# Moving one of three PSUM evacuations of the attention from ScalarE to VectorE, and removing dead parts of the expert value sums

## The chip, the cores and the metric

One core of a Trainium2 chip runs the whole layer in one launch. The metric is the device time of the execution in microseconds (us), of which the median of several runs is taken. A profile is one execution with the hardware profiler on; its span runs from the first to the last instruction.

## What is computed

The reference is one layer of a hybrid backbone over 1024 tokens of width 1024, in float32, with 256 context tokens. The parts that matter here, cut from it:

```python
def one_block(qblk):                       # grouped-query attention: 8 heads, 2 key/value heads, 1280 keys
    s = jnp.einsum('bqkgd,btkd->bkgqt', qblk, k) * scale
    p = jax.nn.softmax(s.astype(jnp.float32), axis=-1).astype(v.dtype)
    return jnp.einsum('bkgqt,btkd->bqkgd', p, v)
...
def chunk(xc):                             # PEER: 128 tokens, 8 heads, the best 16 of 16384 experts per head
    ...
    eidx = jnp.take_along_axis(cidx, pos, axis=-1)
    g = jax.nn.softmax(best, axis=-1)
    a = jnp.einsum('chkd,cd->chk', u_tab[eidx], xc)
    wgt = (jax.nn.gelu(a.astype(jnp.float32)) * g).astype(xc.dtype)
    return jnp.einsum('chk,chkd->cd', wgt, v_tab[eidx])
```

Around them stand a modulated RMSNorm, one input projection, a long convolution (Hyena) beside the attention, gates, an output projection, and a final RMSNorm.

## The kernel before

Tokens lie on 128 partitions, in 8 tiles of 128. The program is written in stages, and a scheduler orders each engine's instructions by simulating a timeline, so stages overlap and one edit can reorder every engine behind it. Each engine then works its own list strictly in that order. The stages and when the trace shows them:

- to 660 us: conditioning, norms, key/value projection, the filters of the convolution, the query projection, and the columns of the convolution and the gates (`hcols`);
- to 870 us: the convolution (`hyena`, lines 180 to 285), of which each spectrum is a block of matmuls and then some twenty VectorE operations (lines 209 to 234);
- 680 to 1200 us: the attention (`attn`, lines 600 to 655), first between the convolution's matmuls, then alone, and from about 940 us between the matmuls of `rest` for tiles 0 to 3 (merge, output projection, expert queries), which fill TensorE;
- 1140 to 1860 us: `rest` for tiles 4 to 7, the selection of the best experts (`topk`), and the dense gate matrices of tiles 0 to 4 (`gbuild`);
- from 1740 us to the end: `dense`, where for tiles 0 to 4 all 16384 experts are computed by matmul, in 32 chunks. Between its steps runs `background`, where tiles 5 to 7 gather their 128 rows of U per token (`usweep`), multiply and reduce them on VectorE, and then gather and add 128 rows of V (`vrows`).

The attention in detail. A step takes one token tile and a pair of heads, one of each key/value head. For each head TensorE computes scores `sc` in three PSUM blocks (line 622), VectorE takes their maxima (`m`, `nmx`, lines 623 and 624), ScalarE exponentiates into `pr` (line 627), TensorE transposes `pr` in groups of 4, 4 and 2 blocks of 128 keys into a PSUM tile `pt` (line 633), and ScalarE copies each group to `pT` in SBUF (line 634). `pt` has two buffers (`npt` is 2), so a third group waits until the first is copied out. Twenty matmuls (line 640) then sum the values, and VectorE copies the result to `aT` (line 641). With 64 heads times tiles there are 192 copies, three per head.

The experts of tiles 5 to 7. `topk(..., False)` ends with the chosen experts' numbers `ef` as floats. Line 855 transposes them on TensorE into the one-buffer PSUM tile `ms`, line 858 casts `ef` to the integers `ei`, which the gathers of lines 887 and 933 use, and line 860 casts the transposed numbers to `eT`. `eT` is read only in `vsweep` (lines 897 to 925), which `background` makes only for a tile outside `VD`; `VD` is (5, 6, 7), which is all of them. So `vsweep` is never run, and the tile `wdz` that it uses is set aside in SBUF and never written. In `topk` a multiplication by `ce` (line 840, GpSimd) stands between a comparison (`eq`, line 839) and a sum (`ef`, line 841) on VectorE.

Of the kernel before, what the change touches and what calls it, by code (L numbers as in the profile page):

```python
# [10 lines left out]
F32 = mybir.dt.float32  # L11
F32R = mybir.dt.float32r
I32 = mybir.dt.int32
# [4 lines left out]
PSUM = bass.MemoryType.PSUM  # L18
# [3 lines left out]
D = 1024  # L22
# [33 lines left out]
CH, WB, VH, GA, UR = 4, 4, 4, 1, 1  # L56
# [8 lines left out]
VD = (5, 6, 7)  # L65
# [4 lines left out]
def body(tc, d, out, dbg=None):  # L70
# [22 lines left out]
    with es:  # L93
# [506 lines left out]
        def attn(tiles, kT, vt, hsel, p, ps, nsc):  # L600
            npt = 2
            blks = ((0, 512), (512, 1024), (1024, 1280))
            for ti in tiles:
# [9 lines left out]
                for h2 in range(4):  # L613
                    pTs = []
                    for kv in range(2):
# [13 lines left out]
                        for k0 in range(0, 10, 4):  # L629
                            nk = min(4, 10 - k0)  # L630
                            pt = ps.tile([128, 512], F32, name="pt", bufs=npt)
                            for m in range(nk):
                                PE.transpose(pt[:, m * 128:(m + 1) * 128], pr[:, (k0 + m) * 128:(k0 + m + 1) * 128], ident)
                            S.copy(pT[:, k0:k0 + nk, :], pt[:, :nk * 128].rearrange("p (m t) -> p m t", m=nk))
# [165 lines left out]
        def topk(i, v16, i16, p, res, ps, dense):  # L800
# [53 lines left out]
            pt = ps.tile([128, 512], F32, name="ms")  # L854
            PE.transpose(pt[:, 0:128], efl, ident)
            if not dense:
                ei = res.tile([128, 128], I32, name=f"ei{i}", bufs=1)
                V.tensor_copy(ei, efl)
                eT = res.tile([128, 128], I32, name=f"eT{i}", bufs=1)
                V.tensor_copy(eT, pt[:, 0:128])  # L860
                tops[i] = gwl, ei, eT
                return
            PE.transpose(pt[:, 128:256], gwl, ident)
# [33 lines left out]
        def vsweep(i, tops, ws, p, gp, ms, ap, res, wdz):  # L897
            w, eT = ws[i], tops[i][2]
            pt = ms.tile([128, 512], F32, name="ms")
            PE.transpose(pt[:, :128], w, ident)  # L900
            acc = ap.tile([128, 2, 512], F32, name="acc")
            pv = pt[:, :128].rearrange("p (c t) -> p c t", c=4)
            wT = res.tile([128, 4, 32], F32, name="wT", bufs=1)
            V.tensor_copy(wT, pv)
            for th in range(8):
                V.memset(wdz, 0.0)
                V.tensor_copy(wdz[:, :, th * 4:128:33], wT[:, :, th * 4:th * 4 + 4])
                for tm in range(4):
                    tl = th * 4 + tm
                    vgs = [gp.tile([128, D], F32, name="row", bufs=RW) if c else p.tile([128, D], F32, name="vg", bufs=VB) for c in range(4)]  # L910
                    for c in range(4):
                        G.indirect_dma_start(out=vgs[c], out_offset=None, in_=d["v"], in_offset=bass.IndirectOffsetOnAxis(ap=eT[:, c * 32 + tl:c * 32 + tl + 1], axis=0))
                    lead = None
                    for h in range(2):
                        for c in (3, 0, 1, 2):
                            mm = PE.matmul(acc[c * 32:c * 32 + 32, h, :], wdz[:, c, tm * 32:tm * 32 + 32], vgs[c][:, h * 512:(h + 1) * 512],
                                           start=tl == 0, stop=tl == 31, tile_position=(0, c * 32))
                            if lead is None:
                                lead = mm
                            else:  # L920
                                tc.add_manual_dep(mm.ins, lead.ins.name, mybir.DependencyInfo(mybir.DependencyClass.NoSync, mybir.DependencyReason.DATA), reason="behind the last gather")
                    yield 1
            gt = [gp.tile([128, D], F32, name="row", bufs=RW) for _ in range(4)]
            gates(gt)
            final(i, acc.rearrange("p a b -> p (a b)"), gt[2], gt[3], gt, p)

# [373 lines left out]
```

## Time and profile before

| | |
|---|---|
| median of 3 runs | 3746.49 us (3746.31 to 3755.15) |
| the profiled execution | 3752.46 us |
| its span | 3750.7 us |
| mean granted TensorE clock | 0.949 |
| TensorE (PE) matmul busy | 3369.1 us, 90% |
| VectorE (DVE) busy | 2879.9 us, 77% |
| ScalarE (ACT) busy | 1445.1 us, 39% |
| GpSimd (POOL) busy | 1709.2 us, 46% |

Shares are means over stages with different limits, so a stage is read from its own stretch. A row of the waits names the waiting engine with its tile and line, then what released it, then the sum of the idle time, the number of waits and the longest. A row of instruction groups gives busy time and the mean length of one in ns, and after the second bar the idle time of that engine just before them. PE is TensorE's matmuls, PEld its weight loads. An arrow points from what is read to what is written, and names stand without their numbers.

### The profile page before, as it was taken

The numbers are of one execution on the slowest core, as the hardware profiler recorded it, in microseconds if no ns is written. First come the engines' busy times: TensorE is split into PE (matmuls) and PEld (weight loads), VectorE is DVE, ScalarE is ACT, GpSimd is POOL, SyncE is SP. The second block draws the span as 40 slices with busy tenths as digits, with TensorE's granted clock in tenths as the row PEclk, the third lists the DMA queues.
The fourth block names the chain that finished last, engine by engine and source line by source line (L and its number), as shares of the span: only waits on it lengthen the run. The fifth ranks groups of instructions, "written<-read, shape, count | busy, mean of one in ns | idle before, by whom it ended". The sixth has DMA issues, their size and how long they took to land.

```text
span 3750.7 us, 53277 instructions
## 1 busy us (share of the span) xinstructions
PE 3369.1 (90%) x19601; PEld 2948.2 (79%) x19601; DVE 2879.9 (77%) x5428; ACT 1445.1 (39%) x2966; POOL 1709.2 (46%) x1360
## 2 busy tenths in 40 slices
PE   5899999789999886998889998999999999799998
PEld 2787888567887676888778888988888888687887
DVE  4655554574446899999897989898898989787777
ACT  5543422446565268885511222222232222122222
POOL 0233133220421465104486767676576666544452
PEclk6999999899999998999989999999999999899999
DMA  4554355863322344434488999999999989888886
GB/s 164 176 165 153 129 202 167 294 226 117 110 85 65 104 141 163 167 141 142 165 305 307 322 327 329 337 344 324 335 342 331 325 317 326 286 286 285 264 281 210
DMA packets 334241, 868.31 MB, mean 232 GB/s; under 512 B 31777, under 2 KB 145377, under 8 KB 324764
## 3 DMA queue, kind: packets, MB, share of 16 engines
q0 software_dynamic: 123904, 453.04, 33.9%
q1 hardware_dynamic: 210076, 411.87, 32.4%
q8 instruction: 154, 2.52, 0.3%
q14 instruction: 107, 0.88, 0.1%
HBM read 777.63 MB, written 87.18 MB: 231 GB/s over the span
## 4 chain that ended last, share of the span: by engine, by line
DVE 23%; DMA 16%; PE 14%; issue 8%; POOL 3%; ACT 2%; SPq 0%; DVEq 0%; POOLq 0%; ACTq 0%
PE mm L85 5%; PE mm L86 4%; PE mm L87 4%; DMA vg<-in_v,ei 4%; DMA vr<-in_v 3%; DVE row L888 3%; DVE acc L937 3%; DMA row<-in_u,ei 3%; DMA ur<-in_uT 3%; DVE o L953 2%; DVE o L965 2%; DVE wl L91 1%; DMA h<-in_v,ei 1%; DVE o L963 1%; POOL row L887 1%
## 5 line engine op out<-in xcount | busy, mean ns | idle before, releaser
L85 PE MATMUL mm<-h2Th,uh 128*128 128x320 f32 x2048 | 644.7, 315 | 60.7 <-ACT uh L90 50.3
L87 PE MATMUL mm<-h2Th,ul 128*128 128x320 f32 x2048 | 638.5, 314 | 26.7 <-DVE ul L91 25.8
L86 PE MATMUL mm<-h2Tl,uh 128*128 128x320 f32 x2048 | 641.7, 314 | 0.0
L887 POOL DMA_INDIRECT row<-in_u,ei x384 | 500.4, 1303 | 192.9 <-issue 75.3
L85 PE MATMUL mm<-vh,wh 128*128 128x512 f32 x1280 | 500.6, 404 | 59.6 <-DVE acc L1022 35.9
L888 DVE SCALAR_TENSOR_TENSOR row<-row,h 128x1024 f32<-128x1024 f32 x384 | 508.1, 1341 | 25.1 <-DMA row<-in_u,ei 21.7
L86 PE MATMUL mm<-vl,wh 128*128 128x512 f32 x1280 | 504.3, 401 | 5.8 <-DVE vl L91 3.9
L87 PE MATMUL mm<-vh,wl 128*128 128x512 f32 x1280 | 497.4, 400 | 7.6 <-DVE wl L91 7.5
L85 PEld LDWEIGHTS mm<-h2Th,uh 128*128 128x128 f32 x2048 | 392.9, 192 | 68.6 <-ACT uh L90 56.0
L933 POOL DMA_INDIRECT vg<-in_v,ei x255 | 310.6, 1218 | 295.8 <-DVE acc L937 244.7
L87 PEld LDWEIGHTS mm<-h2Th,ul 128*128 128x128 f32 x2048 | 389.9, 191 | 34.1 <-DVE ul L91 32.1
L86 PEld LDWEIGHTS mm<-h2Tl,uh 128*128 128x128 f32 x2048 | 392.9, 192 | 1.6
L937 DVE SCALAR_TENSOR_TENSOR acc<-vg,gw,acc 128x1024 f32<-128x1024 f32 x252 | 323.3, 1283 | 60.8 <-DMA vg<-in_v,ei 55.7
L85 PEld LDWEIGHTS mm<-vh,wh 128*128 128x128 f32 x1280 | 247.7, 194 | 124.7 <-DVE acc L1022 46.3
L87 PEld LDWEIGHTS mm<-vh,wl 128*128 128x128 f32 x1280 | 248.3, 194 | 63.9 <-DVE wl L91 10.2
L86 PEld LDWEIGHTS mm<-vl,wh 128*128 128x128 f32 x1280 | 248.7, 194 | 57.2 <-DVE vl L91 5.6
L90 ACT CAST uh<-ur 128x1024 fp32r<-128x1024 f32 (+1 forms) x130 | 137.8, 1060 | 360.4 <-DMA ur<-in_uT 308.8
L90 ACT CAST vh<-vr 128x1024 fp32r<-128x1024 f32 x133 | 139.2, 1047 | 323.9 <-DMA vr<-in_v 207.6
L1040 ACT ACTIVATE ga<-mm 128x320 f32<-128x320 f32 x256 | 107.1, 436 | 395.8 <-PE mm L87 203.0
L91 DVE TENSOR_TENSOR ul<-ur,uh 128x1024 fp32r<-128x1024 f32 (+1 forms) x130 | 165.2, 1271 | 109.0 <-ACT uh L90 102.1
L1022 DVE TENSOR_TENSOR acc<-acc,mm 128x512 f32<-128x512 f32 x322 | 209.9, 680 | 42.3 <-PE mm L87 35.3
L90 ACT CAST wh<-ga 128x640 fp32r<-128x640 f32 (+2 forms) x136 | 94.7, 696 | 373.2 <-DVE ga L1000 232.2
(359 smaller groups left out, 7837.2 us busy)
## 6 DMA issues: line engine op xcount, KB each, us to landing
vr<-in_v SPq DMA_DIRECT2D x133, 512.0 KB
ur<-in_uT SPq DMA_DIRECT2D x128, 512.0 KB
gd<-gst SPq DMA_DIRECT2D x40, 1024.0 KB
gt<-gd SPq DMA_DIRECT2D x32, 1024.0 KB
wt<-in_ada_w SPq DMA_DIRECT2D x12, 2048.0 KB
cfr<-in_cf POOLq DMA_DIRECT2D x32, 512.0 KB
mt<-in_cf POOLq DMA_DIRECT2D x16, 1024.0 KB
mt<-in_ci POOLq DMA_DIRECT2D x16, 1024.0 KB
```

Source lines behind the costliest of these rows:

```text
L85: PE.matmul(ps, ah, bh, start=start, stop=False)
L86: PE.matmul(ps, ah, bl, start=False, stop=False)
L87: PE.matmul(ps, al, bh, start=False, stop=stop)
L90: S.copy(hi, src)
L91: (eng or V).tensor_tensor(lo, src, hi.bitcast(F32), OP.subtract)
L887: G.indirect_dma_start(out=ug, out_offset=None, in_=d["u"], in_offset=bass.IndirectOffsetOnAxis(ap=ei[:, s_:s_ + 1], axis=0))
L888: V.scalar_tensor_tensor(ug, ug, 1.0, h2, OP.mult, OP.mult, accum_out=a[:, s_:s_ + 1])
L933: G.indirect_dma_start(out=row, out_offset=None, in_=d["v"], in_offset=bass.IndirectOffsetOnAxis(ap=ei[:, s_:s_ + 1], axis=0))
L937: V.scalar_tensor_tensor(acc, row, w[:, s_:s_ + 1], acc, OP.mult, OP.add)
L953: V.tensor_tensor(o2, io128[:, None, :].to_broadcast([128, 4, 128]), i2T[:, ts_, None].to_broadcast([128, 4, 128]), OP.is_equal)
L1022: V.tensor_tensor(acc[:, i, h, :], acc[:, i, h, :], po, OP.add)
L1040: S.activation(ga[:, ts_], pa[:, :NS], AF.Gelu_apprx_tanh)
```

## The change

In the attention the middle one of the three copies of a head (`k0 == 4`) is issued on VectorE; the first and third stay on ScalarE. In `topk` the transposition of `ef` is made only for the dense tiles, and `eT` of tiles 5 to 7 is gone. `vsweep`, `wdz`, `VD` go. The PSUM pool of `ms`, one bank, is closed before `dense` begins; the number of PSUM buffers of `dense` gets a name, PB, with the old value 5.

```diff
-CH, WB, VH, GA, UR = 4, 4, 4, 1, 1
+CH, WB, VH, GA, UR, PB = 4, 4, 4, 1, 1, 5
...
-VD = (5, 6, 7)
...
-                            S.copy(pT[:, k0:k0 + nk, :], pt[:, :nk * 128].rearrange("p (m t) -> p m t", m=nk))
+                            (V.tensor_copy if k0 == 4 else S.copy)(pT[:, k0:k0 + nk, :], pt[:, :nk * 128].rearrange("p (m t) -> p m t", m=nk))
...
-            pt = ps.tile([128, 512], F32, name="ms")
-            PE.transpose(pt[:, 0:128], efl, ident)
             if not dense:
                 ei = res.tile([128, 128], I32, name=f"ei{i}", bufs=1)
                 V.tensor_copy(ei, efl)
-                eT = res.tile([128, 128], I32, name=f"eT{i}", bufs=1)
-                V.tensor_copy(eT, pt[:, 0:128])
-                tops[i] = gwl, ei, eT
+                tops[i] = gwl, ei
                 return
+            pt = ps.tile([128, 512], F32, name="ms")
+            PE.transpose(pt[:, 0:128], efl, ident)
...
-        def vsweep(i, tops, ws, p, gp, ms, ap, res, wdz):
...
-                ps = pool("deps", 5, PSUM, stack=st)
+                ps = pool("deps", PB, PSUM, stack=st)
...
-                ms = pool("ms", 1, PSUM, stack=sg, side="right")
+                sm_ = ExitStack()
+                ms = pool("ms", 1, PSUM, stack=sm_, side="right")
...
+                sm_.close()
                 gp = pool("gp", 1, stack=sg, side="right")
...
-                    wdz = vp.tile([128, 4, 128], F32, name="wdz")
-                    vs = [vsweep(i, tops, ws, vp, gp, ms, ap, res, wdz) for i in E if i not in VD]
-                    vs += [vrows(i, tops, ws, vp, gp, ap) for i in VD]
+                    vs = [vrows(i, tops, ws, vp, gp, ap) for i in E]
```

The scheduler orders all engines anew from the first moved copy on. Up to there the lists are the same, and so are the last 2188 instructions of TensorE and the last 339 of VectorE. Three places matter. Line numbers in the rows of the change are its own: one less up to line 855 of the old file, where 633 is the copy, and 33 less in `dense`, where 967 is the old 1000 and 885 is the old 888.

**VectorE, a spectrum of the convolution beside the attention.** `uv` and `t` belong to the convolution, `m`, `nmx`, `aT` and `pT` to the attention. Before:

```order
L212 TENSOR_TENSOR uv<-s_4739 128x2x256
L213 TENSOR_TENSOR uv<-s_4739 128x2x256
L623 TENSOR_REDUCE m_6469<-sc_6474 128x1
L623 TENSOR_REDUCE m_6469<-sc_6478 128x1
L214 TENSOR_TENSOR uv<-s_4739 128x2x256
L215 TENSOR_TENSOR uv<-s_4739 128x2x256
L624 TENSOR_REDUCE nmx<-m_6469 128x1
L641 COPY aT<-pt 128x128
L217 TENSOR_TENSOR t_4747<-uv,kt 128x2048
```

and now:

```order
L622 TENSOR_REDUCE m_6469<-sc_6470 128x1
L622 TENSOR_REDUCE m_6469<-sc_6474 128x1
L622 TENSOR_REDUCE m_6469<-sc_6478 128x1
L213 TENSOR_TENSOR uv<-s_4739 128x2x256
L214 TENSOR_TENSOR uv<-s_4739 128x2x256
L633 COPY pT<-pt 128x512
L623 TENSOR_REDUCE nmx<-m_6469 128x1
L633 COPY pT<-pt 128x512
L216 TENSOR_TENSOR t_4747<-uv,kt 128x2048
```

Two copies of `pT` now stand in VectorE's list behind the convolution's `uv` operations and around `nmx`. Sixteen of the 64 moved copies stand ahead of the convolution's last VectorE operation.

**VectorE, from the last gate matrix to the first row of U.** `ga` and `wl` are the dense part's weighing, `eq` and `ef` the selection for the last tile, `row,a` the first multiplication of `usweep`. Before:

```order
L91 TENSOR_TENSOR vl<-vr,vh 128x1024
L860 CAST eT_18498<-ms 128x128
L841 TENSOR_REDUCE ef<-eq 128x8x4
L841 TENSOR_REDUCE ef<-eq 128x4x4
L91 TENSOR_TENSOR ul<-ur,uh 128x1024
L839 TENSOR_TENSOR eq<-io_9536,pos 128x320
L839 TENSOR_TENSOR eq<-io_9536,pos 128x280
L1000 TENSOR_TENSOR ga<-ga,gt 128x640
L1000 TENSOR_TENSOR ga_29662<-ga_29662,gt_29663 128x128
L91 TENSOR_TENSOR wl<-ga,wh 128x640
L888 SCALAR_TENSOR_TENSOR row,a<-row,h_17427 128x1024
```

and now:

```order
L838 TENSOR_TENSOR eq<-io_9536,pos 128x400
L840 TENSOR_REDUCE ef<-eq 128x2x4
L838 TENSOR_TENSOR eq<-io_9536,pos 128x400
L840 TENSOR_REDUCE ef<-eq 128x2x4
L967 TENSOR_TENSOR ga<-ga,gt 128x640
L840 TENSOR_REDUCE ef<-eq 128x2x4
L967 TENSOR_TENSOR ga_29650<-ga_29650,gt_29651 128x128
L855 CAST ei_19626<-ef 128x128
L90 TENSOR_TENSOR wl<-ga,wh 128x640
L967 TENSOR_TENSOR ga<-ga,gt 128x640
L885 SCALAR_TENSOR_TENSOR row,a<-row,h_17424 128x1024
```

The cast of `eT` is gone. Seven more `eq` and nine more `ef` stand ahead of the first row of U than before, so the selection for the last tile ends here; before, it ended among the rows of U. TensorE has by the last gate matrix 73 more of the dense part's matmuls behind it than before.

**GpSimd at the same place.** `eq` is the selection's multiplication, `row` a gather of U, `vg` one of V. Before:

```order
L840 TENSOR_TENSOR eq<-eq,ce 128x320
L91 TENSOR_TENSOR vl<-vr,vh 128x1024
L887 DMA row<-in_u,ei_17382 128x1024 x7
L840 TENSOR_TENSOR eq<-eq,ce 128x320
L840 TENSOR_TENSOR eq<-eq,ce 128x280
L887 DMA row<-in_u,ei_17382 128x1024 x2
L840 TENSOR_TENSOR eq<-eq,ce 128x280
```

and now:

```order
L839 TENSOR_TENSOR eq<-eq,ce 128x256
L839 TENSOR_TENSOR eq<-eq,ce 128x320 x2
L839 TENSOR_TENSOR eq<-eq,ce 128x280 x4
L839 TENSOR_TENSOR eq<-eq,ce 128x400 x4
L884 DMA row<-in_u,ei_17381 128x1024 x7
L900 DMA vg<-in_v,ei_17381 128x1024 x2
L884 DMA row<-in_u,ei_17381 128x1024 x14
```

All multiplications of the last tile stand ahead of the first gather, where nine came after it before, and two gathers of V follow the first seven of U.

## Rows read from the trace of the kernel before

**Rows 1.** The page's first part: busy time, share of the span and number of instructions of each engine.

```profile
PE 3369.1 (90%) x19601; PEld 2948.2 (79%) x19601; DVE 2879.9 (77%) x5428; ACT 1445.1 (39%) x2966; POOL 1709.2 (46%) x1360
```

**Rows 2.** Busy time by stretch, as the first line says.

```profile
core 0: us, PE busy (x) PEld busy (x) DVE busy (x) ACT busy (x) POOL busy (x), PEclk, DMA share, GB/s
680.00:870.00 190.00, 163.99 (x1256) 125.89 (x1257) 127.35 (x192) 88.37 (x205) 47.75 (x26) 0.93 0.65 231
870.00:1100.00 230.00, 222.61 (x1827) 193.08 (x1826) 99.90 (x213) 142.92 (x356) 61.40 (x46) 0.99 0.32 100
1100.00:1140.00 40.00, 30.44 (x256) 25.34 (x254) 22.54 (x42) 31.18 (x63) 13.23 (x7) 0.87 0.33 112
1140.00:1260.00 120.00, 117.63 (x700) 99.37 (x699) 81.49 (x455) 50.36 (x95) 16.64 (x7) 1.00 0.22 67
1300.00:1855.00 555.00, 473.42 (x3003) 432.10 (x3003) 536.06 (x1744) 405.74 (x1148) 224.22 (x271) 0.93 0.42 147
1855.00:1880.00 25.00, 14.81 (x92) 14.54 (x93) 11.89 (x16) 7.09 (x14) 9.89 (x10) 0.81 0.89 329
1880.00:1920.00 40.00, 30.83 (x111) 23.86 (x110) 40.00 (x64) 3.94 (x7) 31.82 (x25) 0.82 0.84 279
1920.00:3700.00 1780.00, 1653.60 (x8956) 1484.18 (x8954) 1521.82 (x1838) 417.67 (x597) 1095.55 (x804) 0.97 0.89 314
```

**Rows 3.** TensorE's waits from 680 to 1200 us.

```profile
PE pt L633 <- ACT pT L634: 17.4, 23, 2.9
PE pt L633 <- ACT pr L627: 9.1, 3, 4.5
PE sc L622 <- ACT pr L627: 8.0, 6, 2.4
...
PE pt L640 <- ACT pT L634: 1.9, 4, 0.8
```

**Rows 4.** The first of them in the second part of the stretch, from 870 to 1200 us.

```profile
PE pt L633 <- ACT pT L634: 12.7, 14, 2.9
```

**Rows 5.** ScalarE's copies of `pT`, and, from the dense part, VectorE's copy of a PSUM block of the same shape: shortest, median and longest in ns.

```profile
L634 ACT COPY pT<-pt x192: 354/586/640, 683.2 to 1187.8; 128x512 f32<-128x512 f32 x128, 128x256 f32<-128x256 f32 x64
L1020 DVE COPY acc<-mm x10: 627/672/683, 1742.8 to 1931.8; 128x512 f32<-128x512 f32 x10
```

**Rows 6.** VectorE's groups from 680 to 870 us.

```profile
L217 DVE TENSOR_TENSOR t<-uv,kt 128x2048 f32<-128x2048 f32 x4 | 14.4, 3594 | 0.0
...
L222 DVE TENSOR_TENSOR yz<-t 128x1024 f32<-128x1024 f32 x4 | 4.9, 1223 | 3.2 <-POOL t L220 3.1
...
L209 DVE TENSOR_TENSOR s<-px,ys 128x1024 f32<-128x1024 f32 x4 | 4.9, 1215 | 7.0 <-PE px L87 7.0
```

**Rows 7.** VectorE's instructions in order of time about 1867 us: start, length, instruction, and in brackets the idle time before it.

```profile
1858.62 1.23 DVE L91 TENSOR_TENSOR vl<-vr,vh 128x1024 fp32r<-128x1024 f32 x1 [0.66 <-ACT vh L90]
1867.16 0.29 DVE L860 CAST eT<-ms 128x128 int32<-128x128 f32 x1 [7.32 <-PE ms L855]
...
1871.58 0.82 DVE L1000 TENSOR_TENSOR ga<-ga,gt 128x640 f32<-128x640 f32 x1
1874.23 1.28 DVE L1000 TENSOR_TENSOR ga<-ga,gt 128x128 f32<-128x128 f32 x1 [1.83 <-DMA gt<-gd]
...
1876.85 1.23 DVE L888 SCALAR_TENSOR_TENSOR row<-row,h 128x1024 f32<-128x1024 f32 x1
```

**Rows 8.** GpSimd's instructions at the same time, in the same columns.

```profile
1851.10 2.81 POOL L91 TENSOR_TENSOR vl<-vr,vh 128x1024 fp32r<-128x1024 f32 x1
1865.34 1.03 POOL L887 DMA_INDIRECT row<-in_u,ei  x1 [11.44 <-DMA gd<-gst]
```

**Rows 9.** TensorE's waits from 1855 to 1925 us.

```profile
PE mm L85 <- ACT ga L1040: 10.2, 1, 10.2
PE mm L85 <- DVE acc L1022: 5.3, 1, 5.3
PE mm L87 <- DVE wl L91: 3.8, 2, 3.0
```

**Rows 10.** The selection's groups from 1700 to 1960 us: GpSimd's `eq`, VectorE's `eq` and `ef`.

```profile
L840 POOL TENSOR_TENSOR eq<-eq,ce 128x280 f32<-128x280 f32 (+3 forms) x42 | 45.7, 1093 | 53.0 <-DVE eq L839 51.2 <-PE ms L970 1.7
...
L839 DVE TENSOR_TENSOR eq<-io,pos 128x280 f32<-128x280 f32 (+3 forms) x42 | 30.8, 741 | 1.5 <-POOL ce L817 1.5
...
L841 DVE TENSOR_REDUCE ef<-eq 128x8 f32<-128x280 f32 (+3 forms) x44 | 20.9, 482 | 0.9 <-POOL eq L840 0.9
```

**Rows 11.** TensorE's transpositions of `ef`, of which three of the eight are taken out.

```profile
L855 PE MATMUL ms<-ident,ef x8: 272/300/449, 1324.9 to 1940.4; 128*128 128x128 f32 x8
```

More of the change, by code (lines that the diff above doesn't have):

```diff
@@ L895, in usweep @@
             ws[i] = gw
-        def vsweep(i, tops, ws, p, gp, ms, ap, res, wdz):
[L898 to L925, printed above, removed]
         def vrows(i, tops, ws, p, gp, ap):
@@ L931, in vrows @@
             for s_ in range(128):
-                row = gp.tile([128, D], F32, name="h2" if i == 7 else "row", bufs=1 if i == 7 else RW) if s_ % 3 == 1 else p.tile([128, D], F32, name="vg", bufs=VB)
+                row = gp.tile([128, D], F32, name="h2" if i == E[-1] else "row", bufs=1 if i == E[-1] else RW) if s_ % 3 == 1 else p.tile([128, D], F32, name="vg", bufs=VB)
                 G.indirect_dma_start(out=row, out_offset=None, in_=d["v"], in_offset=bass.IndirectOffsetOnAxis(ap=ei[:, s_:s_ + 1], axis=0))
@@ L1179, in tk_ @@
                     def tk_(i):
-                        return topk(i, v16[:, i % 4], i16[:, i % 4], tk, res, ms, False)
+                        return topk(i, v16[:, i % 4], i16[:, i % 4], tk, res, None, False)
                     yield from tk_(E[0])
```

## The prediction

> **What bounds the kernel now.** The page's busy shares come first [rows 1]: TensorE's matmuls are busy 90% of the span, ScalarE 39%, VectorE 77%. That is an average over stages, so the next view is busy time by stretch [rows 2], where the reader should look for the engine that is nearly full in each. From 680 to 870 us, attention beside the convolution, nobody is full: TensorE works 164.0 of 190 us, VectorE 127.4, ScalarE 88.4. From 870 to 1100 us TensorE works 222.6 of 230 us, from 1100 to 1140 us only 30.4 of 40, and to 1260 us it is full again. From 1300 to 1855 us VectorE is the limit, 536.1 of 555 us. At 1855 to 1880 us everybody waits: TensorE 14.8, VectorE 11.9 of 25 us. From 1880 to 1920 us VectorE is full and TensorE works 30.8 of 40. From 1920 us on TensorE works 1653.6 of 1780 us, with the DMA engines at 0.89 of their time: here matmuls, gathers and row products are all close to full, and the change removes none of them.
>
> So the change can shorten the time in two places only: where TensorE waits inside the attention, and at the seam near 1860 us. A shortening of either moves everything after it, because behind the attention stands a stretch in which VectorE always has work, and behind the seam one in which TensorE does.
>
> **The copies.** 64 of the 192 copies go to VectorE, all of the 128x512 form. On ScalarE the median copy takes 586 ns; VectorE's copy of a PSUM block of that shape takes 672 ns [rows 5]. ScalarE thus sheds 64 x 0.586 = 37.5 us and VectorE takes on 64 x 0.672 = 43.0 us. Neither counts by itself: ScalarE has no shortage of time in these stretches (88.4 + 142.9 + 31.2 = 262.5 us in 460, 57%), and VectorE goes from 127.4 + 99.9 + 22.5 = 249.8 us to some 293 in the same 460. What hides the 43 us is VectorE's idle time, and if that cover were gone (as after 1300 us, where it is 97% busy) they would count in full; no copy lies there.
>
> What counts is TensorE's waits in the stretch [rows 3]. For copies of `pT` it waits 17.4 + 1.9 = 19.3 us, for exponentials 9.1 + 8.0 = 17.1 us. With two buffers of `pt`, the third group of transposes waits for the first copy and the next head's first group for the second. Three copies in a row on ScalarE become two on it and one beside them, so the chain of a head falls from three copies to two at most, and if the exponentials don't stand between, TensorE should get its buffer one copy sooner. I take half of the copy waits, 9.7 us, since the first copy of a head, for which the third group waits, is not moved. Of the exponentials' waits I take the share by which ScalarE's work falls, 37.5 of 262.5 or 14%, so 2.4 us.
>
> Against that stands a new wait. VectorE works its list in order, and 16 of the moved copies stand among the convolution's operations. VectorE was busy 67% of 680 to 870 us with 192 operations of 0.66 us on average [rows 2]; a copy that meets one in progress at random waits half of it, 0.22 us with the 67%, and 16 of them 3.5 us. Behind a waiting copy are queued the maxima and `nmx` of the next head, and for these ScalarE's exponentials wait. Net: 9.7 + 2.4 - 3.5 = 8.6 us gained. The bounds are wide. The best is that all 36.4 us of both kinds of waits go. The worst is that each of the 16 copies stands behind the convolution's longest operation, 3.594 us [rows 6], and TensorE with it: 57.5 us lost. I choose near the average operation because the new order puts only some of them directly behind the long ones; the first row of the waits was mostly paid after 870 us, 12.7 of 17.4 us [rows 4], where no such operation is left.
>
> The Trainium skill, page "Perfetto Trace Analysis", section "Identifying the Most-Contended Engine", says to find the engine with the highest occupancy and improve that one first. ScalarE is not that engine in any stretch here; by that rule alone the copies would give nothing and the sum below would be 8.2 us instead of 16.8. The waits above are what the trace shows against it, and the rule is a rival below.
>
> **The seam.** At 1859.8 us VectorE comes to the cast of `eT` and sits 7.32 us until TensorE's transposition, which stands behind a run of dense matmuls, is done [rows 7]. Nothing reads `eT`. With it gone VectorE's next work is the selection for the last tile, and the new order puts 7 more `eq` and 9 more `ef` ahead of the first row of U: 7 x 0.741 + 9 x 0.482 = 9.5 us of VectorE's work [rows 10] that before stood in 1880 to 1920 us, where VectorE was full and TensorE lost 9.1 us to it and 10.2 us before [rows 9]. GpSimd's nine multiplications that move ahead of the first gather are 9 x 1.093 = 9.8 us [rows 10] and fit in its 11.44 us of waiting for `gst` [rows 8]; past that point two gathers of V come earlier, each about as long as one of U, 1.03 us, on a queue that was idle there. I take 7.3 us, the removed wait, as the least of 7.3, 9.5 and 9.1. It may give nothing, since the dense part there also waits for its gate matrix (1.83 us before the second `ga` [rows 7]) and for rows of U; if the multiplications all delayed the gathers it would lose 9.8 us; at most it gives 19.3 us, all of TensorE's waits there.
>
> **The rest.** Three transpositions of 0.3 us on TensorE and three casts of 0.285 us on VectorE [rows 7, 11] go; I count VectorE's 0.9 us. `vsweep` and `wdz` issued nothing, and the freed bank and space are given to nobody: 0. That the order of the long dense part changes in detail I put at 0, with 10 us either way as an estimate: TensorE is idle 126 us of the 1780 there [rows 2], and 8% of that is what a different interleaving could move. The last third is in the same order.
>
> **Sum.** 8.6 + 7.3 + 0.9 = 16.8 us. The profiled execution took 3752.46 us, 6 us above the median 3746.49; it becomes 3735.7, and the median about 3729.7. About 0.3% (11 us) is what a measurement of this kernel can tell from no change.
>
> **The rivals.**
>
> *Nothing reaches the end.* Between 940 and 1100 us and from 1140 to 1260 us TensorE is full because `rest` fills its waits, so a faster attention may only move that filler; and what the seam gives may be taken back by gathers and loads, with the DMA engines at 0.89 from 1920 us on [rows 2]. This is also where the skill's rule above would lead. For it: ScalarE's low share. Against it: TensorE's matmuls are a fixed amount and its idle time before 1260 us is real. With half of the seam's 8.2 us left it gives 3746.5 - 4.1 = 3742. Chance 0.27.
>
> *VectorE's list becomes the attention's wait.* In 680 to 870 us the copies stand behind the convolution's `uv`, `t` and `yz`, and TensorE, which has the next transposes at the head of its own list, stands with them. By the mean of the three kinds of rows [rows 6], (3.594 + 1.223 + 1.215) / 3 = 2.0 us, 16 copies cost 32 us; the later attention still gains half of 12.7 us and the seam 7.3 and 0.9, so the time rises by 32 - 6.4 - 8.2 = 17.4 to 3764. It decides when a copy beside the convolution costs TensorE more than (11 + 14.6) / 16 = 1.6 us. For it: VectorE's list has no way around a long operation. Against it: the maxima of the same heads already stand there, so TensorE waited for that list before, and 26 us of TensorE's time in this stretch was idle anyway. Chance 0.14. The skill, page "PSUM — Partial Sum Buffer", section "Engine vs sequencer instructions", calls the queues of ScalarE, VectorE and GpSimd strict first in, first out. The 7.32 us before the cast of `eT` agree, since work that was ready stood behind it; applied to the copies the rule gives this rival, at 3764 instead of 3730.
>
> *Much more.* All waits of TensorE on ScalarE in the attention go and the seam gives all of its 19.3 us: 36.4 + 19.3 + 0.9 = 56.6 us, 3690; with half of that surplus over the forecast, 3710. Chance 0.09.
>
> **How the numbers follow.** The forecast, 3730, has the remaining chance of 0.50, and I put within it 8 to 28 us of gain. Faster by over 0.3% needs 3735: nearly all of the forecast and the third rival, 0.46 + 0.09 = 0.55. Within 0.3%: the first rival and the small end of the forecast, 0.27 + 0.04 = 0.31. Slower: 0.14, the second rival. The range reaches from 3702, which takes in half of the surplus of the third rival, to 3754, which takes in the first with the 10 us of order against it; outside lie most of the second and the far end of the third.
>
> **What would show it.** Right: TensorE's waits for `pT`, now on ScalarE and VectorE together, fall from 19.3 to some 10 us; the projections behind the attention end at about 1251 instead of 1260 us; VectorE has no wait near 7 us at the seam and the first row of U comes some 10 us earlier; from there to the end the two traces keep their distance. Wrong: a row of TensorE waiting for VectorE's `pT` of over 25 us between 680 and 870 us (second rival); an attention that ends sooner while the seam does not (first rival); or a distance that grows or shrinks by more than 10 us after 1920 us, which would mean that the new order of the dense part counts for more than both edits.

## The result: 36.5 us slower, and the profile after

The changed kernel takes **3782.83 us** (median of 5, 3779.37 to 3792.83) beside 3746.31 us of the kernel before (median of 5, 3744.14 to 3755.15): a ratio of 1.0096, 95% interval 1.0077 to 1.0116. The forecast was 3730, the range ended at 3754. The profiled execution took 3783.29 us with a span of 3781.5, 30.8 more than before, and the two spans are compared here.

The busy line of the page, to answer [rows 1]. ScalarE sheds 32.5 us and VectorE takes on 46.8, near the 37.5 and 43.0 of the prediction:

```profile
PE 3379.5 (89%) x19598; PEld 2956.6 (78%) x19598; DVE 2926.7 (77%) x5489; ACT 1412.6 (37%) x2901; POOL 1725.1 (46%) x1360
```

Where the time went is found by laying landmarks of VectorE's timeline side by side: the ninth copy of `aT`, which ends the first step of the third tile (in both kernels after all matmuls of the convolution); the start of the last squared sum `sa` of the projections; and the start of the last product `o<-io,i2T` of the gate matrices (line 953 before, 920 after).

| from, to | before | after | difference |
|---|---|---|---|
| span's start to the ninth attention step | 869.5 | 890.1 | +20.6 |
| to the last `sa` (the projections fill the attention's waits) | 481.7 | 477.4 | −4.3 |
| to the last `o`, "the stretch" below | 499.3 | 520.6 | +21.3 |
| to the end, "the dense part" below | 1900.2 | 1893.4 | −6.8 |

(The texts on record call that copy the eighth step; it is the same moment.) So there are two losses of some 20 us each, one among the first of the moved copies and one behind the last of them. The convolution itself is hardly late: its last VectorE operation starts at 870.0 us in place of 868.5. It is the attention beside it that falls behind.

**First loss.** Busy time up to that step and over the eight steps after it, first before, then after. The columns are those of [rows 2].

```profile
680.00:869.51 189.51, 163.50 (x1254) 125.49 (x1255) 126.99 (x191) 87.88 (x205) 47.75 (x26) 0.93 0.65 232
869.51:947.04 77.53, 70.14 (x603) 55.81 (x602) 37.53 (x85) 57.50 (x150) 7.34 (x5) 0.96 0.36 116
```

```profile
680.00:890.15 210.15, 171.79 (x1249) 132.55 (x1247) 138.45 (x209) 76.56 (x177) 52.49 (x30) 0.89 0.64 222
890.15:972.11 81.96, 69.19 (x595) 57.71 (x594) 42.77 (x97) 48.43 (x134) 2.37 (x1) 0.92 0.19 62
```

TensorE does the same matmuls up to the step (within six rows of some 4390), but is idle for 38.4 us in place of 26.0, and busy for 8.3 us more at a granted clock of 0.89 in place of 0.93. Idle time and a slower clock come together here. Its waits up to the step, before and after:

```profile
PE pt L633 <- ACT pr L627: 9.1, 3, 4.5
PE pt L633 <- ACT pT L634: 4.7, 9, 0.7
PE pt L144 <- DVE aT L641: 3.2, 1, 3.2
PE sc L622 <- ACT pr L627: 2.9, 2, 2.4
...
PE pt L633 <- DVE nmx L624: 1.3, 1, 1.3
```

```profile
PE pt L632 <- ACT pr L626: 7.3, 3, 4.8
PE pt L632 <- DVE pT L633: 6.1, 3, 3.4
PE pt L632 <- ACT pT L633: 6.1, 10, 0.7
PE pt L632 <- DVE nmx L623: 5.6, 2, 3.9
PE px L84 <- ACT pr L626: 3.2, 1, 3.2
...
PE pt L632 <- DVE bt L144: 1.8, 1, 1.8
```

With the small rows not shown, waits on VectorE rise from 6.9 to 17.0 us, those on ScalarE from 18.6 to 20.6. One of them is this, and with it what ScalarE waits for next (start, length, instruction, idle time before):

```profile
745.67 0.69 PE L632 MATMUL pt<-ident,pr 128*128 128x128 f32 x2 [3.36 <-DVE pT L633]
749.47 0.69 ACT L626 ACTIVATE pr<-sc,nmx 128x512 f32<-128x512 f32 x1 [2.70 <-DVE nmx L623]
```

The transposes that the two copies read are done by 742.1 us. VectorE's list, without a gap, has them later:

```profile
738.88 2.79 DVE L211 TENSOR_TENSOR uv<-s 128x512 f32<-128x512 f32 x1
741.60 0.68 DVE L212 TENSOR_TENSOR uv<-s 128x512 f32<-128x512 f32 x1
742.21 1.27 DVE L622 TENSOR_REDUCE m<-sc 128x1 f32<-128x512 f32 x2
...
744.94 1.27 DVE L633 COPY pT<-pt 128x512 f32<-128x512 f32 x2
746.13 3.17 DVE L216 TENSOR_TENSOR t<-uv,kt 128x2048 f32<-128x2048 f32 x1
749.23 0.14 DVE L623 TENSOR_REDUCE nmx<-m 128x1 f32<-128x3 f32 x1
```

Two copies stand behind the convolution's `uv` and the maxima, and TensorE waits for them. Behind the copies stand `t` and then the negated maximum, and ScalarE's exponentials wait for that: the picture that the second rival drew. It is one of the waits; that the others are of this kind is not shown.

**Second loss.** Between the last `sa` and the last `o` no copy lies, and VectorE works off nearly the same instructions, in another order. A split below is the division of numbers into a high and a low part (`wh` on ScalarE, `wl` on VectorE or GpSimd). Take the middle of the stretch, from the first `FIND_INDEX8` of the second four tiles to the last (149.6 us before, 157.5 after). VectorE's groups and GpSimd's one, before:

```profile
L793 DVE FIND_INDEX8 i<-v,so 128x8 uint32<-128x128 f32 x128 | 34.2, 280 | 0.0
L953 DVE TENSOR_TENSOR o<-io,i2T 128x512 f32<-128x512 f32 x43 | 29.0, 674 | 0.0
L963 DVE TENSOR_SCALAR o<-io,i1T,gT 128x128 f32<-128x128 f32 x56 | 17.6, 374 | 0.9 <-PE ms L970 0.9
L91 POOL TENSOR_TENSOR wl<-wr,wh 128x1024 fp32r<-128x1024 f32 x6 | 14.2, 2368 | 110.0 <-DVE so L795 38.4 <-ACT wh L90 35.6 <-DVE v L792 18.5
```

and after:

```profile
L792 DVE FIND_INDEX8 i<-v,so 128x8 uint32<-128x128 f32 x128 | 34.2, 278 | 0.0
L920 DVE TENSOR_TENSOR o<-io,i2T 128x512 f32<-128x512 f32 x42 | 32.1, 763 | 0.0
L930 DVE TENSOR_SCALAR o<-io,i1T,gT 128x128 f32<-128x128 f32 x56 | 23.6, 480 | 0.0
L90 POOL TENSOR_TENSOR wl<-wr,wh 128x1024 fp32r<-128x1024 f32 x6 | 23.6, 3939 | 105.7 <-ACT wh L89 88.1 <-PE ms L937 17.6
```

The `o` operations are longer by 3.1 + 6.0 us, GpSimd's six splits by 1.6 us each; the searches cost the same. The timelines show where. Before, GpSimd's splits start beside the searches:

```profile
1543.11 2.37 POOL L91 TENSOR_TENSOR wl<-wr,wh 128x1024 fp32r<-128x1024 f32 x1 [21.45 <-DVE so L795]
1543.03 0.86 DVE L792 MAX8 v<-so 128x8 f32<-128x128 f32 x4
1543.87 0.28 DVE L793 FIND_INDEX8 i<-v,so 128x8 uint32<-128x128 f32 x1
```

After, they start beside the products (the last row is two of the 374 ns kind, in 2.64 us; the split ends at 1570.77):

```profile
1567.13 3.64 POOL L90 TENSOR_TENSOR wl<-wr,wh 128x1024 fp32r<-128x1024 f32 x1 [18.16 <-ACT wh L89]
1567.27 0.68 DVE L920 TENSOR_TENSOR o<-io,i2T 128x512 f32<-128x512 f32 x1
1567.87 0.68 DVE L932 TENSOR_TENSOR o<-io,i1T 128x512 f32<-128x512 f32 x1
1568.47 2.64 DVE L930 TENSOR_SCALAR o<-io,i1T,gT 128x128 f32<-128x128 f32 x2
```

In each of the six splits one `o` operation takes 2.39 to 2.58 us and ends 0.1 to 0.6 us after the split; it alone is long. The products that start earlier beside the same split keep their 0.67 us, and counted from the start of the long one the split lasts 2.0 to 2.3 us, near its 2.37 of before. It reads as if the split first waited for the run of products, and then the next operation for the split. Before, five of the `o` operations meet the end of a split and take 0.38 to 1.2 us.

The middle is 7.9 of the 21.3 us; 2.8 lie ahead of it and 10.7 behind it, up to the last `o`. Of these, 6.2 are more idle time of VectorE, which waits longer for splits of ScalarE (4.5 us before) and for GpSimd's `eq` (0.9 before), and 4.5 are more busy time, of which the cause was not followed up:

```profile
DVE ul L90 <- ACT uh L89: 9.0, 2, 4.8
DVE ef L840 <- POOL eq L839: 4.1, 7, 0.9
```

### The profile page after: what moved, and what is told of

Its sections match the earlier page's. It is cut to its first block, busy times and chain, and to the rows that moved or that the text cites. A ratio compares the mean times of both kernels' runs of the same rounds, so it can differ in the third digit from the quotient of the medians.

```text
span 3781.5 us, 53312 instructions
## 1 busy us (share of the span) xinstructions
PE 3379.5 (89%) x19598; PEld 2956.6 (78%) x19598; DVE 2926.7 (77%) x5489; ACT 1412.6 (37%) x2901; POOL 1725.1 (46%) x1360
## 4 chain that ended last, share of the span: by engine, by line
DVE 26%; PE 19%; DMA 18%; issue 9%; POOL 5%; ACT 2%; SPq 1%; DVEq 0%; POOLq 0%; another core or an unknown queue 0%; ACTq 0%
DVE row L885 4%; PE mm L84 4%; PE mm L86 4%; PE mm L85 4%; DMA ur<-in_uT 4%; DMA vg<-in_v,ei 4%; DVE acc L904 4%; DMA vr<-in_v 3%; DMA row<-in_u,ei 3%; DMA h<-in_v,ei 2%; DVE wl L90 2%; DVE o L920 2%; POOL row L884 2%; DVE o L932 2%; PE sc L621 1%
## 5 line engine op out<-in xcount | busy, mean ns | idle before, releaser
L989 DVE TENSOR_TENSOR acc<-acc,mm 128x512 f32<-128x512 f32 x322 | 210.3, 681 | 23.4 <-PE mm L86 22.8
```

Source lines behind the costliest of these rows:

```text
L989: V.tensor_tensor(acc[:, i, h, :], acc[:, i, h, :], po, OP.add)
```

## The experiments

Theory A: copies on VectorE delay the attention, because they stand in its list. Theory O: the scheduler, given another attention, orders the later stretches anew, and each order has its own length, copies or not. All spans and stretches below are of one profiled execution each; timed runs of one kernel scatter by 10 to 15 us either way, so a ratio and a span can disagree by that much (by 19 us in e12). Columns: the ninth step, the last `sa`, the stretch, the dense part, the ratio to before in timed runs.

| kernel | step | last `sa` | stretch | dense | ratio, 95% |
|---|---|---|---|---|---|
| before | 869.5 | 1351.2 | 499.3 | 1900.2 | |
| after | 890.1 | 1367.5 | 520.6 | 1893.4 | 1.0096, 1.0077 to 1.0116 |
| e1 copies alone | 886.9 | 1367.3 | 518.9 | 1877.3 | 1.0044, 1.0027 to 1.0061 |
| e2 removal alone | 870.4 | 1356.4 | 496.0 | 1894.0 | 0.9997, 0.9984 to 1.0010 |
| e3 copies from tile 3 on | 870.1 | 1349.0 | 519.0 | 1896.2 | 1.0046, 1.0028 to 1.0064 |
| e4 last copy instead | 885.4 | 1360.9 | 505.2 | 1896.5 | 1.0054, 1.0035 to 1.0073 |
| e5 copies in tiles 1, 2 | 888.8 | 1382.1 | 492.7 | 1903.6 | 1.0080, 1.0048 to 1.0111 |
| e6 a quarter of the copy | 889.6 | 1360.9 | 520.6 | 1902.5 | 1.0097, 1.0065 to 1.0128 |
| e7 after, RB0 = 1 | 893.2 | 1373.6 | 502.7 | 1901.9 | 1.0065, 1.0044 to 1.0086 |
| e8 before, RB0 = 1 | 870.3 | 1358.8 | 508.0 | 1905.1 | 1.0031, 1.0013 to 1.0049 |
| e9 removal, sixth bank | 873.2 | 1355.5 | 454.3 | 1957.5 | 1.0060, 1.0037 to 1.0084 |
| e10 after, t1 in halves | 886.6 | 1365.5 | 518.7 | 1892.5 | 1.0067, 1.0044 to 1.0089 |
| e11 before, t1 in halves | 869.5 | 1353.6 | 517.6 | 1871.3 | 0.9985, 0.9971 to 1.0000 |
| e12 removal, t1 in halves | 865.6 | 1348.9 | 516.7 | 1892.3 | 1.0070, 1.0046 to 1.0094 |
| e13 half as many copies | 881.1 | 1355.9 | 502.9 | 1897.5 | 1.0039, 1.0021 to 1.0058 |
| e14 twice as many copies | 884.4 | 1379.9 | 490.8 | 1904.2 | 1.0107, 1.0075 to 1.0139 |

**e1 and e2, one part each.** e1 is before with

```
-S.copy(pT[:, k0:k0 + nk, :], pt[:, :nk * 128].rearrange("p (m t) -> p m t", m=nk))
+(V.tensor_copy if k0 == 4 else S.copy)(pT[:, k0:k0 + nk, :], pt[:, :nk * 128].rearrange("p (m t) -> p m t", m=nk))
```

> The kernel before with one edit: the middle copy of each head (k0 == 4) on VectorE; the dead cast eT and its bank stay. Theory A (VectorE's list delays the attention): by the end of the eight attention steps beside the convolution, near 870 us, the attention is about 20 us behind the kernel before, after the attention about 28 us, and after the projections behind it about 17 us, as in the changed kernel; the end is 17 us or more later, 3763 or above. If the copies carry also the second loss of about 18 us between 1290 and 1893 us, 3780. Theory B (the removal's new order costs what is lost after 1290 us): 3763 here, and the distance to the kernel before stays at 17 us from 1290 us on. Theory C (the copies help and all the loss is the removal): 3738.

e2 takes the same line back out of after.

> The changed kernel with the middle copy back on ScalarE: only the dead value sums, the cast of eT and its transposition are gone. Theory A alone: the attention is that of the kernel before to 1 us, the wait of 7.3 us at the seam is gone, 3738 to 3746. Theory B (the removal's new order costs 18 us between 1290 and 1893 us): 3764. Theory C: 3783.

The copies alone carry both losses (+16.1 us at the last `sa`, +19.6 in the stretch) and then win 22.9 in the dense part; the removal alone costs and gives nothing. The two ratios, +0.44% and 0, do not add up to 0.96%: what the removal changes once the copies are there is the dense part, from 1877.3 to 1893.4. Theory C and theory B as they stood are out.

**e3 and e5, where the copies count.** After with the condition of the copy changed, in e3 and in e5:

```
-(V.tensor_copy if k0 == 4 else S.copy)
+(V.tensor_copy if k0 == 4 and ti >= 2 else S.copy)
+(V.tensor_copy if k0 == 4 and ti < 2 else S.copy)
```

> The changed kernel with the middle copy on VectorE only from the third tile of the attention on, so that the 16 copies beside the convolution are on ScalarE again. Theory A in the form that the convolution's long operations are the price: the attention is level with the kernel before at 870 us, within 4 us, loses at most 8 us in the pure steps after it, and the end is 25 to 35 us earlier than the changed kernel's if only the attention carries the loss, 3750 to 3760. If it is the place between the maxima and the negated maximum that costs, wherever the copy stands: half or more of the attention's loss stays, 3765 or above.

> The changed kernel with the middle copy on VectorE only in the first two tiles of the attention, beside the convolution: the counterpart of the run with the copies from the third tile on. Theory A (VectorE's list and the clock that falls with the longer idle time): the eighth attention step ends 18 to 22 us later than before, and the pure steps after it lose nothing, within 2 us. Theory O (the new order of 1350 to 1890 us is what costs the second half, copies or not): this kernel has a third order there, and the stretch from the last squared sum of the projections to the last outer product may take anything from 495 to 522 us (497 to 500 in the two kernels that have the old order, 519 to 521 in the three that have the new one). Rival: copies on VectorE lengthen that stretch by themselves, 519 or more here too.

With the 16 copies beside the convolution back on ScalarE the step is level with before (870.1), and with these alone it is at 888.8: the first loss is theirs. Three misses. e3 is 20 us better than after and not 25 to 35, since VectorE's list in the stretch is the changed kernel's to the last instruction, and the length with it. In e5 the eight steps after the ninth take 83.5 us, 6 more than before, without a copy on VectorE in them; TensorE was busy for 74.8 us there in place of 70.1, with ten more matmul rows. And the stretch of e5 is 492.7 us, below the 495 set down for a third order; the rival, 519 or more, is out all the same.

**e4 and e6, is it the copy's length?** The first line in e4, the others in e6, both from after:

```
-(V.tensor_copy if k0 == 4 else S.copy)
+(V.tensor_copy if k0 == 8 else S.copy)
...
+kv_ = 1 if k0 == 4 else 0
+if kv_:
+    V.tensor_copy(pT[:, k0:k0 + 1, :], pt[:, :128].rearrange("p (m t) -> p m t", m=1))
+S.copy(pT[:, k0 + kv_:k0 + nk, :], pt[:, kv_ * 128:nk * 128].rearrange("p (m t) -> p m t", m=nk - kv_))
```

> The changed kernel with the last copy of a head (k0 == 8, 128x256) on VectorE in place of the middle one (k0 == 4, 128x512). If a copy's own length on VectorE is the price (0.67 us each, half of it here), the attention loses half as much, 14 us instead of 28. If the wait behind VectorE's list is the price, the loss at the end of the steps beside the convolution is again about 20 us. Where the last copy stands later than the middle one, the value sums wait for it instead of the transposes: 3770 to 3785 by that reading, 3765 by the first.

> The changed kernel with the middle copy split: its first block of 128 columns on VectorE, the other three on ScalarE. VectorE's time for 64 copies falls from 43 us to about 19 (0.29 us each by the 128x128 copies of this kernel), ScalarE has nearly all of its own back. If VectorE's time for the copies is the price, the eighth attention step is 6 to 9 us later than before; if their place in its list is (the transposes and the negated maxima stand behind the convolution's long operations whatever the copy's length), 15 us or more, as with the whole copy (21 us).

The half-length copy costs 15.9 us at the step, the quarter 20.1: the loss does not fall with the length. Both prove less than they were meant to. e4 moves another group of the head, and comes out between its two readings (10 or 20 us at the step; 3766.67 us beside 3765 or 3770 and more). In e6 ScalarE's part waited for VectorE's, 5.8 us up to the step and more behind it, in a row of the whole attention that after does not have:

```profile
ACT pT L636 <- DVE pT L635: 23.7, 20, 3.0
```

**e13 and e14, 8 and 32 copies in place of 16.** The condition in e13 and in e14:

```
-(V.tensor_copy if k0 == 4 else S.copy)
+(V.tensor_copy if k0 == 4 and kv == 0 else S.copy)
+(V.tensor_copy if k0 < 8 else S.copy)
```

> The changed kernel with the middle copy on VectorE only for the first of the two heads of a step (kv == 0): 8 copies beside the convolution in place of 16. Theory A (a price per copy of about 1.3 us, 20.6 us by 16): the eighth attention step ends about 10 us after that of before, 7 to 13. Rival (the order that any such edit brings): 0 to 4, or 17 and more.

> The changed kernel with the first and the middle copy of each head on VectorE (k0 of 0 and 4): 32 copies beside the convolution. Theory A: the eighth step ends 35 to 45 us after that of before, and in the pure steps, where VectorE has 40 of 77 us free, it loses under 15. Rival: about 20, as with 16 copies, since the waits are already there.

Against 0, 8, 16 and 32 copies the step is late by 0, 11.6, 20.6 and 14.9 us. The first three lie on a line, the fourth does not: with 32 copies TensorE's waits on VectorE's `pT` alone are 12.9 us up to the step, but those on ScalarE, with two copies of three gone, are 10.7 in place of 20.6 with 16. So a fixed price per copy is refuted; both readings of e14 missed. What stands is that every set of copies tried there makes the step 11.6 to 23.7 us late, and that without them it comes at 865.6 to 873.2 us. How much of that is the place in VectorE's list and how much the order that TensorE gets with it stays open.

**e10 and e11, the longest operation cut in two.**

```
-V.tensor_tensor(t1, uv, kt, OP.mult)
+V.tensor_tensor(t1[:, 0:4], uv[:, 0:4], kt[:, 0:4], OP.mult)
+V.tensor_tensor(t1[:, 4:8], uv[:, 4:8], kt[:, 4:8], OP.mult)
```

> The changed kernel with the convolution's longest operation on VectorE, the product t1 of 128x2048 (3.2 us and more, 8 times), written as two halves of 128x1024, so that a copy or a negated maximum may pass between. If a single long operation in front of them is what the attention waits for, TensorE's idle time up to the eighth attention step falls from 38 us towards 30 and the step ends 5 to 8 us earlier than in the changed kernel. If it is the whole list (copies, maxima and some 20 operations of the convolution in a row), it stays at 36 to 40 us. Theory O: the order of 1350 to 1890 us is the changed kernel's, so the stretch takes 519 to 523 us again.

> The kernel before with the same two halves of t1, no copy moved and nothing removed. The attention is that of before to 3 us (TensorE's idle time 24 to 26 us up to the eighth step). By this edit the order of 1350 to 1890 us comes close to the changed kernel's, with every copy on ScalarE. Theory O (the order of that stretch is the cause): 515 to 522 us for the stretch in place of 500, and 3755 to 3770 for the whole. Rival (copies on VectorE, or the later end of the attention, lengthen it): 496 to 503 us and 3745 to 3753.

In e10 the step comes at 886.6 us and TensorE is idle for 36.9 us until then; e1 has 886.9 and 36.3 with the operation whole, so it is not one long operation. e11 is the run that settles the second loss. Every copy is on ScalarE, the attention ends as before, yet the order of the stretch is close to the changed kernel's (1392 of VectorE's 1605 operations in sequence, where before has 745) and its length is 517.6 us. Busy time in the middle of the stretch, in after and in e11: VectorE without a gap, and GpSimd's six splits 23.6 and 23.5 us long in place of 14.2.

```profile
1553.90:1711.73 157.83, 146.59 (x906) 130.70 (x905) 157.83 (x654) 134.38 (x406) 23.63 (x6) 0.98 0.36 131
```

```profile
1539.00:1697.00 158.00, 146.55 (x907) 130.69 (x905) 157.99 (x655) 134.49 (x407) 23.49 (x6) 0.97 0.36 131
```

That the whole run is not slower, against the expectation, is the dense part: 1871.3 us, in the order that e1 has, row for row on VectorE (1877.3 there).

**e7 and e8, another order by one number behind the attention.**

```
-RB, RB0, RBR, MGB = 3, 2, 1.0, 4
+RB, RB0, RBR, MGB = 3, 1, 1.0, 4
```

> The changed kernel with one number changed that stands behind the attention: the dense weights begin after one part of the second projections in place of two (RB0 = 1). Attention and VectorE's copies are those of the changed kernel up to its end, 32 us later than before. Theory O: the order of 1350 to 1890 us is a new one, and the stretch's 521 us can change by up to 20 either way though no copy moves; a time 10 us or more off the changed kernel's 3783 is expected. Rival (the copies lengthen the stretch by themselves, or a later attention does): 519 to 523 us again and 3783.

> The kernel before with the same one number changed (RB0 = 1), no copy moved and nothing removed. Theory O: its stretch from the last squared sum to the last outer product differs from the 500 us of before by 8 us or more although the attention is the same. Rival (only copies on VectorE lengthen it): 496 to 503 us, 3741 to 3752.

With all 64 copies on VectorE the stretch falls from 520.6 to 502.7, with none it rises from 499.3 to 508.0. The rival, that copies lengthen it by themselves, is out. The time is only 7 us below the changed kernel's in e7, less than expected, because the projections end 6 us later and the dense part takes 8.5 more.

**e12, a time forecast from the orders alone.** Removal and halves together, each free by itself.

> The kernel before with the dead value sums and the cast of eT removed and t1 in two halves: neither edit cost anything alone (3748 and 3747 us beside 3749 to 3751 of before), and every copy is on ScalarE. The order of its dense part, from the last outer product on, is the changed kernel's row for row on VectorE, and that of 1350 to 1890 us nearly the changed kernel's. Theory O (each stretch has the length of its order): the end of the projections at 1353 us as in the run with the halves alone, 519 us of stretch, 1892 us to the end, so a span near 3764, and 3760 to 3770 in the timed runs: slower than before by 0.4% with no copy on VectorE. Rival (edits that cost nothing alone cost nothing together): 3745 to 3752.

The stretch is 516.7 and the dense part 1892.3, near the forecast; the span, 3757.9, is 6 us short since the projections end 4 us earlier and the stretch is 2 us shorter. The timed runs are slower, 3775.26 us or 1.0070: a kernel with no copy on VectorE, nothing but dead code removed and one operation cut in two is 0.7% slower than before. The profiled execution, 3759.66 us, was the fastest of the eight, so the lengths account for 7 us of span, and the rest of the 0.7% is not explained.

**e9, the freed bank put to use.** e2 with

```
-CH, WB, VH, GA, UR, PB = 4, 4, 4, 1, 1, 5
+CH, WB, VH, GA, UR, PB = 4, 4, 4, 1, 1, 6
```

> The changed kernel with the middle copy back on ScalarE and the bank that the removal frees given to the long dense part (PB = 6 in place of 5). In the run with the removal alone TensorE waits there 46.8 us, 18 times, for a bank that VectorE has yet to empty. If the sixth bank takes half of these waits and they are not replaced by waits for weights or rows: 20 us faster than the removal alone, 3728. If the weights' splits (40 us of waits there) or the rows of U and V bound it anyway: 3745, within 8 us.

Neither: 0.6% slower. The scheduler moves work past the last `o` (stretch 454.3, dense 1957.5), together 22 us more than e2's. No version beats the kernel before by more than its measurement can tell.

## Why the prediction was wrong, point by point

- **What bounds the kernel** held: TensorE's waits in the attention, VectorE after it. The sentence that the change "can shorten the time in two places only" failed, because it asked where the change acts and not what the scheduler does with it. The stretch from 1350 to 1890 us, with 536.1 of 555 us busy [rows 2], was read as a fixed sum of work; its length is that of an order, 490.8 to 520.6 us in the fifteen kernels with five banks. One reading was off too: the prediction has ScalarE as the busiest engine in no stretch, and from 1100 to 1140 us it is, with 31.2 us against TensorE's 30.4 [rows 2].
- **The copies, durations:** right. ScalarE lost 32.5 us of the 37.5, VectorE gained 46.8 with the 64 copies in it, 691 ns each in the median where 672 was set down.
- **The copies, term +8.6: the step that failed first.** The price of the 16 copies in VectorE's list, 3.5 us or 0.22 each, was 20.6 or 1.3 each: the mean operation was taken where the list puts copies behind several, and nothing was set down for the clock, 8.3 us of it. Of the gain of 9.7 us in copy waits, 2.1 came: waits for `pT` on both engines fall from 19.3 to 17.2 us from the start of the attention to 1290 us. Up to the ninth step they rise from 6.6 to 13.5; behind it they do fall, from 12.7 to 3.8, but there TensorE's waits for exponentials rise from 5.2 to 11.3 us, where 2.4 in all were to go. VectorE, which now copies too, has the negated maxima later, and ScalarE waits for them. Its waits from the ninth step to 1290 us, before and after (with copies on VectorE there, in e1, e3 and e14, they are 22.8 to 37.9 us, without, in e2, e5 and e11, 4.1 to 8.0):

```profile
ACT pr L627 <- DVE nmx L624: 7.8, 10, 2.5
ACT pr L626 <- DVE nmx L623: 25.9, 25, 3.5
```

  The projections' end, forecast 9 us earlier, is 16.3 later.
- **The seam, term +7.3:** the 7.32 us wait is gone [rows 7], but the first row of U comes 24.7 us after the start of the last `o` in place of 26.4: 1.7 us. VectorE's time there went to the selection for the last tile, from 1889.3 to 1908 us, and the weighing `ga` of the gate matrix stands behind it, at 1907.1. The prediction had named the gate matrix as what could take the gain. TensorE's wait for it grew from 10.2 us [rows 9] to

```profile
PE mm L84 <- ACT ga L1007: 18.0, 1, 18.0
```

  The wait was one of that order and not of the cast itself: in e1, where the cast still stands, VectorE reaches it without a wait, and the first row of U comes 20.5 us after the last `o`.

```profile
1892.29 0.28 DVE L860 CAST eT<-ms 128x128 int32<-128x128 f32 x1
```

- **Order of the dense part, 0 ± 10:** the whole dense part, the seam in it, is 6.8 us shorter, near the 8.2 of the forecast but not by its mechanism, so that is luck. With five banks it is 1871.3 to 1905.1 us, from 29 below to 5 above the kernel before, so a bound of 10 was too narrow.
- **Order of the stretch:** no term at all, and +21.3 us. With the copies' term (8.6 us forecast as gain, 16.3 lost at the projections' end, an error of 24.9) it makes up nearly all of the error of 47.6 us in the span, 16.8 less forecast and 30.8 more measured. The stretch alone would have left the time inside the range, at 3751; the copies' term alone would have put it just past its end, at 3755.
- **The rivals.** The second had the mechanism of the first loss, its place, and by chance the time of the copies alone: 3764 against the 3763.41 us of e1. Its point of decision, 1.6 us for each copy, was not reached by the 1.3 measured, and its sign in the trace was a bad one: TensorE's wait on VectorE's `pT` is 6.5 us and not 25, because the same list holds up more than copies: the exponentials, by way of `nmx`, and at 761 us TensorE's longest wait put down to `nmx` (3.9 us), which ends just as `bt` does, an addition of the conditioning that reads a `pt` buffer and stands behind six of the convolution's operations. Part of the loss is the lower clock. The gain of half of 12.7 us in the later attention, which it shared with the forecast, came as 8.9 us of copy waits and went again as 6.1 of exponentials.
- **The two rules of the Trainium skill** set against the trace: the strict queues ("PSUM — Partial Sum Buffer", "Engine vs sequencer instructions") pointed to the loss, and the trace at 745 us agrees. The occupancy rule ("Perfetto Trace Analysis", "Identifying the Most-Contended Engine") would, as the prediction applied it, have had no change from the copies; they cost 0.44%.

## What to carry to other kernels

Where a scheduler writes the engines' lists, an edit is priced in two parts: what it does in its own stretch, and what new order it draws for all that follows, which here was worth from 8 us less to 21 us more in a stretch that one engine fills. The second part can be compared before anything runs, list against list, and measured by an edit that changes the order and nothing else; three kernels with the same list of VectorE (after, e3, e10) had the same length within 2 us in the stretch, and in the dense part e1 and e11, again with one list, were 6 us apart. Work moved to an engine with idle time is not free when that engine's list is strict and another engine's next step needs the result.

## What the runs showed of the hardware

VectorE and GpSimd slow each other here only for some operations. Beside six splits of GpSimd, searches (`FIND_INDEX8`, 280 and 278 ns) are not slowed and do not slow GpSimd (2368 ns each). Beside products of the index rows GpSimd's split goes to 3939 ns; the products go from 674 to 763 and from 374 to 480 ns in the mean, but nearly all of it is one operation of 2.39 to 2.58 us for each split. The Trainium skill, "GPSIMD Engine Reference", "Specifications", says that GpSimd's SBUF interfaces are shared with VectorE, with contention from VectorE's operations with two SBUF inputs or in a 2-port mode; the longer products and the longer splits agree with it, and the rows add which neighbours GpSimd does not disturb. Under which of the two cases the products fall, no run here tells.

The middle of the stretch, 150 us long, came out as 149.6, 149.6 and 149.7 us in before, e2 and e9, and as 157.5 to 157.6 in after, e1, e3, e10, e11 and e12: less than 0.1 us apart within either group, on different chips. In the other seven kernels it was 149.1 to 160.3 us.
